# Two chunk slots instead of three, and two projections moved beside the token groups

## The chip, the core and the metric

The kernel runs on one core of a Trainium2 chip. The metric is the device time of one execution in microseconds (us), median of the runs. Five engines work side by side, each through its own instructions in order: TensorE (PE; its weight loads are listed as PEld), VectorE (DVE), ScalarE (ACT), GpSimd (POOL) and SyncE (SP), which here issues nearly all DMAs.

## The reference

One layer of a decoder step for 1024 prompt tokens and 32 sample tokens (T = 1056 columns) of width 1024, in float32:

```python
n1 = rmsnorm(x, norm_mix_g);  z = n1 @ w_in
y_r, shift_new, wkv_new = rwkv7_mix(z[..., :D_SHIFT], ...)
y_p, pool_new = pool_mix(z[..., D_SHIFT:], ...)
h = x + concatenate([y_r, y_p], -1) @ w_out
h = h + peer_ffn(rmsnorm(h, norm_ffn_g), wq, keys, u, v)
gate = sigmoid(rmsnorm(h, norm_ple_g) @ ple_gate_w)
h = h + (p @ ple_w) * gate
y = rmsnorm(h, final_norm_g)
```

`rwkv7_mix` is a recurrence over tokens with an 8-head state. `pool_mix` is a windowed mean with a small projection. `peer_ffn` scores 16384 experts by two sets of 128 keys, takes the top 16 for each of 8 heads, and mixes the rows of `u` and `v`. Besides y the states are returned.

## The kernel before, in words

Matrices are kept transposed: 128 features on the partitions, tokens as columns. A wide float32 product is made of three matmuls in a reduced format: every operand is split into a high part (ScalarE copy) and a low part (raw minus high, on VectorE or GpSimd), and hi x hi, hi x lo and lo x hi are added up (`mm3`, L651).

1. *Projection* (`phase_a`, L195): z for all columns, the factors of the recurrence, which go to DRAM (`fd`), the pooled half `yp_d`, and split copies of `w_out`'s first half and of `wq` to DRAM (`wc_d`).
2. *Chunks* (`bchunk`, L462): the recurrence in 16 chunks of 64 prompt tokens and one sample chunk. A chunk is a generator of 19 steps of small matmuls (64 columns), each followed by a ScalarE, VectorE or GpSimd instruction whose result the next step needs. The state tile S links the chunks. `b_stream` (L915) runs them round robin: at most NSLOT = 3 at a time, each with tiles of its own slot (`wt`, L472, tag with `slot`), a new one not earlier than STAG = 6 rounds after the last. The sample chunk uses slot 1, and chunks of that slot are held back meanwhile (`sample`, L933).
3. *Two more products*. `ple` (L1004): p @ ple_w, 8 blocks of 128 features x 1056 columns in three parts of XW = 352, to `pl_d`, read only near the end of the kernel. `wpool` (L1021): x plus the pooled half's part of w_out, 8 blocks of 3 parts, to `hx_d`, read by each group.
4. *Groups* (`phase_c`, L678): four token groups of 288, 256, 256 and 256 columns (the first has the 32 sample columns and chunks 0 to 3). Per group: load `y_d` (L687) and `hx_d` (L690), 8 blocks of w_out's first half (L699), norm, 16 blocks of wq (L737), keys, scores to DRAM. `wblock` (L637) loads the split weights, three buffers deep.
5. *Top experts* (`top`, `select`, `t_stream`): VectorE searches of the scores of a group, and the build of dense gates for the first 672 columns (L898 to L907: VectorE and GpSimd make one-hot operands, TensorE multiplies them).
6. *Dense experts and the tail*: from about 1410 us on, wide matmuls over all experts (`emm`, L1104), gathers for the other 384 columns beside them, and the last norm.

The order of the work is written by `merge` (L950), which takes the stream that is least far by its length, and a scheduler then places the instructions of that program order by a timeline of its own. Before the change the streams are:

```python
 960 BC = (0, 2, 4, 5, 8, 12, 16)
 976 merge([(16, A), (b_len(*BC[0:2]), b_stream(*BC[0:2]))])
1048 merge([(30, sample(bchunk(-1, ...))), (b_len(*BC[1:3]), b_stream(*BC[1:3]))])
1049 merge([(KB * (1 + T // XW), (x for st in (ple(), wpool()) for x in st)), (b_len(*BC[2:4]), b_stream(*BC[2:4]))])
1124 for step in range(1, NG + 1):   # streams of a step: chunks BC[step+2:step+4], top of group step-2, phase_c(step-1)
```

So step 1 has group 0 beside chunks 5 to 7, step 2 group 1 beside chunks 8 to 11 and the top search of group 0, and so on. PSUM tiles: `PS("b0")` is one ring of four, used by the chunks; `PS("b2")` and `PS("b3")` have two each.

Of the kernel before, what the change touches and what calls it, by code (L numbers as in the profile page):

```python
# [16 lines left out]
ALU = mybir.AluOpType  # L17
# [45 lines left out]
def body(ctx, tc, io):  # L63
# [63 lines left out]
    def PS(tag):  # L127
        return pools[tag].tile([128, 512], F32, name="ps", tag="bc" if tag in ("b0", "b1") else tag)
# [332 lines left out]
    maxn = max(b - a for a, b in GROUPS)  # L461
    def bchunk(c, sp=None):  # L462
        smpl = sp is not None
        slot = 1 if smpl else c % NSLOT
        pst = "b0"
        tt = NSMP if smpl else 64
        ts = slice(NP, T) if smpl else slice(64 * c, 64 * c + 64)
# [2 lines left out]
        msk = mask4 if smpl else mask64  # L470

        def wt(name, n, bufs=1):  # L472
            return pb.tile([128, n], F32, name=name, tag=f"{name}{slot}", bufs=bufs)

        def q4(name, bufs=1):
            return v3(wt(name, 256, bufs), 64)
# [430 lines left out]
            nc.sync.dma_start(g_d[:, :, (col + t1 - GA) // TC].rearrange("g p e t -> p g e t"), st.rearrange("p (g e) t -> p g e t", e=GQ))  # L907

    NG = len(GROUPS)
    NSLOT = 3  # L910
    STAG = 6

    active, nxt, since, held = [], [0], [0], [False]

    def b_stream(ca, cb, ahead=2):  # L915
        while nxt[0] < cb or any(c < cb for c, _ in active):
            c = nxt[0]
            if (c < min(cb + ahead, NCH) and len(active) < NSLOT and (not active or since[0] >= STAG)
                    and not (held[0] and c % NSLOT == 1)):
                active.append((c, bchunk(c)))  # L920
                nxt[0], since[0] = c + 1, 0
            since[0] += 1
            for a in list(active):
                try:
                    next(a[1])
                except StopIteration:
                    active.remove(a)
                yield

    def b_len(ca, cb):  # L930
        return (cb - ca) * 19

    def sample(g):  # L933
        held[0] = True
        yield from g
        held[0] = False

    def t_stream(gi):
        for t0, m in tiles_of(gi):
# [21 lines left out]
    with tc.tile_pool(name="pa1", bufs=1) as pa1:  # L961
# [13 lines left out]
        bzero()  # L975
        merge([(16, A), (b_len(*BC[0:2]), b_stream(*BC[0:2]))])

    with tc.tile_pool(name="smp", bufs=1) as sp_, tc.tile_pool(name="hx", bufs=1) as hx:
        bm = sp_.tile([128, 32], F32, name="bm")
        nc.gpsimd.affine_select(bm, ones[:, 0:32], pattern=[[-NS, 32]], base=0, channel_multiplier=1,  # L980
                                compare_op=ALU.is_ge, fill=0.0)
        nc.gpsimd.affine_select(bm, bm, pattern=[[NS, 32]], base=NS - 1, channel_multiplier=-1,
                                compare_op=ALU.is_ge, fill=0.0)
        bmask = sp_.tile([128, NB], F32, name="bmask")
        TT(bmask, bm[:, 0:NB], bm[:, 16:16 + NB], op=ALU.add)
        cmask = sp_.tile([128, NB, 64], F32, name="cmask")
        nc.gpsimd.memset(cmask, 1.0)
        nc.gpsimd.affine_select(cmask, cmask, pattern=[[-NS, NB], [1, 64]], base=0, channel_multiplier=0,
                                compare_op=ALU.is_ge, fill=0.0)
        nc.gpsimd.affine_select(cmask, cmask, pattern=[[NS, NB], [-1, 64]], base=NS - 1, channel_multiplier=0,  # L990
                                compare_op=ALU.is_ge, fill=0.0)
        ssm = sp_.tile([128, 4, NB, 64], F32, name="ssm")
        nc.sync.dma_start(ssm, io["state_wkv"])
        pT = sp_.tile([128, 2, T], F32, name="pT")
        nc.sync.dma_start(pT, io["p"])

        def split(pool, raw, shape, nm, bufs):
            hi = pool.tile(shape, F32R, name=nm + "hi", bufs=bufs)
            ACT(hi, raw, AF.Copy)
            lo = pool.tile(shape, F32R, name=nm + "lo", bufs=bufs)  # L1000
            TT(lo, raw, hi.bitcast(F32), op=ALU.subtract)
            return hi, lo

        def ple():  # L1004
            phi, plo = split(sp_, pT, [128, 2, T], "p", 1)
            for db in range(KB):
                wp = sp_.tile([128, 2, 128], F32, name="wp", bufs=2)
                nc.sync.dma_start(wp, io["ple_w"][db])
                hi, lo = split(sp_, wp, [128, 2, 128], "w", 2)
                pss = [PS("b3"), PS("b3"), PS("b2")]  # L1010
                for k in range(2):
                    for w, x, first, last in ((hi, phi, k == 0, False), (hi, plo, False, False), (lo, phi, False, k == 1)):
                        for i, ps in enumerate(pss):
                            mm(ps[:, :XW], w[:, k, :], x[:, k, i * XW:(i + 1) * XW], start=first, stop=last)
                for i, ps in enumerate(pss):
                    o = sp_.tile([128, XW], F32, name="pout", bufs=2)
                    ACT(o, ps[:, :XW], AF.Copy)
                    nc.sync.dma_start(pl_d[:, db, i * XW:(i + 1) * XW], o)
                yield

        def wpool():  # L1021
            yhi = hx.tile([128, PB, T], F32R, name="yhi")
            ylo = hx.tile([128, PB, T], F32R, name="ylo")
            for g in range(PB):
                raw = hx.tile([128, T], F32, name="yraw", bufs=1)
                nc.sync.dma_start(raw, yp_d[:, g, :])
                ACT(yhi[:, g, :], raw, AF.Copy)
                TT(ylo[:, g, :], raw, yhi[:, g, :].bitcast(F32), op=ALU.subtract)
            for b in range(KB):
                raw = hx.tile([128, HK, 128], F32, name="wraw", bufs=2)  # L1030
                nc.sync.dma_start(raw, io["w_out"][b, :, HK:, :])
                hi = hx.tile([128, HK, 128], F32R, name="whi", bufs=2)
                ACT(hi, raw, AF.Copy)
                lo = hx.tile([128, HK, 128], F32R, name="wlo", bufs=2)
                TT(lo, raw, hi.bitcast(F32), op=ALU.subtract)
                for i in range(T // XW):
                    cs = slice(i * XW, (i + 1) * XW)
                    x = hx.tile([128, XW], F32, name="x", bufs=3)
                    nc.sync.dma_start(x, io["x"][:, b, cs])
                    ps = PS("b2")  # L1040
                    mm3(ps, [(hi, lo)], (yhi[:, :, cs], ylo[:, :, cs]), XW)
                    TT(x, ps[:, :XW], x, op=ALU.add)
                    nc.sync.dma_start(hx_d[:, b, cs], x)
                    yield

        spf = sp_.tile([128, 28, 64], F32, name="spf")
        nc.gpsimd.memset(spf, 0.0)
        merge([(30, sample(bchunk(-1, ((sp_, ssm), bmask, cmask, spf)))), (b_len(*BC[1:3]), b_stream(*BC[1:3]))])
        merge([(KB * (1 + T // XW), (x for st in (ple(), wpool()) for x in st)), (b_len(*BC[2:4]), b_stream(*BC[2:4]))])


    tk = phases.enter_context(tc.tile_pool(name="tk", bufs=1, reuse_waits="tile"))
    cstack = ExitStack()
    ws = cstack.enter_context(tc.tile_pool(name="ws", bufs=2))
    mv = cstack.enter_context(tc.tile_pool(name="mv", bufs=1))
    work = cstack.enter_context(tc.tile_pool(name="wc", bufs=1))
# [67 lines left out]
    for step in range(1, NG + 1):  # L1124
        streams = []
        if step < NG:
            c_ = BC[step + 2:step + 4]
            streams.append((b_len(*c_), b_stream(*c_)))
        if 0 <= step - 2 < NG:
            streams.append((t_len(step - 2), t_stream(step - 2)))  # L1130
        if 0 <= step - 1 < NG:
            streams.append((CL[step], phase_c(step - 1)))
        if step == NG:
            for _ in streams[0][1]:
                pass
# [4 lines left out]
        merge(streams)  # L1140
# [278 lines left out]
```

## Time and profile before

| what | value |
|---|---|
| median of 3 runs | 3349.01 us (3345.77 to 3352.56) |
| the profiled execution, its own time | 3365.37 us |
| its span | 3363.7 us |
| mean granted TensorE clock | 0.968 |

The span runs from the first to the last instruction of the profiled execution. Its own time is 16.4 us above the median of the runs, so differences are made against the profiled execution and then set on the median. Times in the rows are from the span's start. A matmul's listed duration includes its latency, and matmuls overlap; what one costs in a stream is a stretch divided by its count.

### The profile page before, as it was taken

The numbers are of one execution on the slowest core, as the hardware profiler recorded it, in microseconds if no ns is written. First come the engines' busy times: TensorE is split into PE (matmuls) and PEld (weight loads), VectorE is DVE, ScalarE is ACT, GpSimd is POOL, SyncE is SP. The second block draws the span as 40 slices with busy tenths as digits, with TensorE's granted clock in tenths as the row PEclk, the third lists the DMA queues.
The fourth block names the chain that finished last, engine by engine and source line by source line (L and its number), as shares of the span: only waits on it lengthen the run. The fifth ranks groups of instructions, "written<-read, shape, count | busy, mean of one in ns | idle before, by whom it ended". The sixth has DMA issues, their size and how long they took to land.

```text
span 3363.7 us, 66962 instructions
## 1 busy us (share of the span) xinstructions
PE 3145.6 (94%) x26777; PEld 3006.4 (89%) x26777; DVE 2585.2 (77%) x5124; ACT 1128.8 (34%) x1734; POOL 1736.5 (52%) x1439
## 2 busy tenths in 40 slices
PE   8997799896998988899999999999999999999997
PEld 7886688786787877899999999999999999999997
DVE  6766322229799879899898888888889888888966
ACT  6452322223555555431221222222222222222243
POOL 5433232215446455327666665566566566666634
PEclk9998899997999989999999999999999999999998
DMA  4668544665776796739999999999999999999933
GB/s 160 203 219 195 145 130 127 204 191 149 235 217 201 232 317 204 244 109 371 343 330 332 343 349 328 333 334 339 337 336 349 326 330 342 338 329 337 323 107 127
DMA packets 448856, 879.89 MB, mean 262 GB/s; under 512 B 110240, under 2 KB 233376, under 8 KB 444064
## 3 DMA queue, kind: packets, MB, share of 16 engines
q1 hardware_dynamic: 337952, 472.91, 43.8%
q0 software_dynamic: 110592, 402.70, 32.9%
q8 instruction: 210, 3.44, 0.4%
q14 instruction: 102, 0.84, 0.1%
HBM read 754.89 MB, written 120.60 MB: 260 GB/s over the span
## 4 chain that ended last, share of the span: by engine, by line
PE 54%; DVE 7%; DMA 2%; issue 1%; ACT 0%; POOL 0%; SPq 0%; ACTq 0%; DVEq 0%; POOLq 0%
PE pd L1110 53%; DVE ab L898 1%; DMA row<-u,idx 1%; DVE elo L1088 1%; DVE oh L850 0%; DMA scq<-sc_d 0%; DMA eraw<-wq 0%; DVE OT L1316 0%; DVE ab L899 0%; DVE I L766 0%; DVE s L768 0%; DVE tg L1302 0%; DVE I L770 0%; DMA g_d<-gst 0%; DMA gq<-g_d 0%
## 5 line engine op out<-in xcount | busy, mean ns | idle before, releaser
L1219 POOL DMA_INDIRECT row<-v,idx x384 | 530.6, 1382 | 330.8 <-DVE po L1236 150.9
L1219 POOL DMA_INDIRECT row<-u,idx x384 | 542.5, 1413 | 274.9 <-DVE row L1227 107.4
L1086 ACT ACTIVATE ehi<-eraw 128x1024 fp32r<-128x1024 f32 x278 | 294.5, 1060 | 1095.9 <-PE pd L1110 976.8
L1110 PE MATMUL pd<-XH,elo 128*128 128x336 f32 x2176 | 515.3, 318 | 5.9 <-POOL elo L125 4.7
L1110 PE MATMUL pd<-XL,ehi 128*128 128x336 f32 x2176 | 515.1, 317 | 0.0
L1110 PE MATMUL pd<-XH,ehi 128*128 128x336 f32 x2176 | 512.4, 316 | 0.4 <-ACT ehi L1086 0.4
L1110 PE MATMUL pd<-wh,ehi 128*128 128x336 f32 (+1 forms) x2112 | 504.1, 317 | 6.6 <-DVE tg L1300 6.2
L1110 PE MATMUL pd<-wl,ehi 128*128 128x336 f32 (+1 forms) x2112 | 504.0, 317 | 0.0
L1110 PE MATMUL pd<-wh,elo 128*128 128x336 f32 (+1 forms) x2112 | 503.9, 317 | 0.2 <-DVE elo L1088 0.2
L1236 DVE SCALAR_TENSOR_TENSOR po<-row,act,po 128x1024 f32<-128x1024 f32 x381 | 488.5, 1282 | 6.8
L1227 DVE SCALAR_TENSOR_TENSOR row<-row,xt 128x1024 f32<-128x1024 f32 x384 | 455.7, 1219 | 9.7 <-DMA row<-u,idx 9.5
L1110 PEld LDWEIGHTS pd<-XH,elo 128*128 128x128 f32 x2176 | 373.5, 188 | 7.1 <-POOL elo L125 5.5
L1088 DVE TENSOR_TENSOR elo<-eraw,ehi 128x1024 fp32r<-128x1024 f32 x256 | 318.3, 1243 | 77.2 <-ACT ehi L1086 69.0
L1110 PEld LDWEIGHTS pd<-XH,ehi 128*128 128x128 f32 x2176 | 372.9, 189 | 0.9 <-ACT ehi L1086 0.6
L1110 PEld LDWEIGHTS pd<-XL,ehi 128*128 128x128 f32 x2176 | 371.3, 188 | 0.2
L1110 PEld LDWEIGHTS pd<-wh,ehi 128*128 128x128 f32 x2112 | 362.6, 188 | 7.6 <-issue 7.4
L1110 PEld LDWEIGHTS pd<-wh,elo 128*128 128x128 f32 x2112 | 362.7, 188 | 0.6 <-DVE elo L1088 0.5
L1110 PEld LDWEIGHTS pd<-wl,ehi 128*128 128x128 f32 x2112 | 362.8, 188 | 0.0
L125 POOL TENSOR_TENSOR ab<-ab,e 128x512 f16<-128x512 f16 x110 | 130.1, 1185 | 180.6 <-DVE ab L899 139.0
L657 PE MATMUL ps<-hi,whi 128*128 128x256 f32 (+1 forms) x592 | 185.7, 315 | 29.3 <-DMA whi<-wc_d 15.8
L1179 DVE TENSOR_TENSOR OT<-pd,OT 128x672 f32<-128x672 f32 x120 | 102.9, 857 | 140.7 <-PE pd L1110 139.8
L905 ACT ACTIVATE gst<-ps 128x512 f32<-128x512 f32 x168 | 174.9, 1089 | 85.5 <-PE ps L903 78.4
(428 smaller groups left out, 5526.9 us busy)
## 6 DMA issues: line engine op xcount, KB each, us to landing
eraw<-uT SPq DMA_DIRECT2D x128, 512.0 KB
eraw<-vP SPq DMA_DIRECT2D x128, 512.0 KB
g_d<-gst SPq DMA_DIRECT2D x21, 2048.0 KB
gq<-g_d SPq DMA_DIRECT2D x32, 1344.0 KB
whi<-wc_d SPq DMA_DIRECT2D x148, 256.0 KB
wlo<-wc_d SPq DMA_DIRECT2D x148, 256.0 KB
fdc<-fd SPq DMA_DIRECT2D x16, 896.0 KB
wc_d<-shi SPq DMA_DIRECT2D x40, 256.0 KB
```

The costliest lines, as they stand in the source:

```text
L125: nc.gpsimd.tensor_tensor(out, a, b, op=op)
L657: mm(ps[:, :n], whi[:, kk, :], xhi[:, k, :n], start=k == 0, stop=False)
L898: TT(ab[:, 0:4], iota16[:, None, :, :].to_broadcast([128, 4, EB, 2]), pairs(0, 4), op=ALU.is_equal)
L905: ACT(st[:, :, t2:t2 + 4].rearrange("p e t -> p t e"), v3(ps, 128), AF.Copy, scale=1.0 / GS)
L1086: ACT(hi, raw, AF.Copy)
L1088: sub(lo, raw, hi.bitcast(F32), op=ALU.subtract)
L1110: mm(ps[:, a, :n], w_[:, k, :], x_[:, s:s + n], start=first, stop=last)
L1179: TT(halves(OT[db]), ps[:, :, :NH], halves(OT[db]), op=ALU.add)
L1219: nc.gpsimd.indirect_dma_start(out=r[:m], out_offset=None, in_=io[tab], in_offset=bass.IndirectOffsetOnAxis(ap=idx[:m, hh, k:k + 1], axis=0))
L1227: STT(r[:m], r[:m], 1.0, xt[:m], op0=ALU.mult, op1=ALU.mult, accum_out=pre[:m, k:k + 1])
L1236: STT(po[:m], r[:m], act[:m, k:k + 1], po[:m], op0=ALU.mult, op1=ALU.add)
```

## The change

The slots go from three to two (STAG 6 to 9), and the sample chunk gets tiles of its own, in its own pool. `wpool` takes a list of column ranges, loads and splits its weights in each call with one buffer each, and is called three times: for group 0's columns (256 prompt and 32 sample columns) beside chunk 4, and for prompt columns 256 to 640 and 640 to 1024 in step 1, beside group 0. `ple` takes a column range, splits on GpSimd and is called three times (352 columns each) in step 2, beside group 1. Both use the chunks' PSUM ring. The pools of the groups (`tk`, `ws`, `mv`, `work`) are opened before the pools of the sample chunk and of `wpool`.

```diff
-        slot = 1 if smpl else c % NSLOT
+        slot = "s" if smpl else c % NSLOT
+        own = sp[0][0] if smpl else pb
...
-            return pb.tile([128, n], F32, name=name, tag=f"{name}{slot}", bufs=bufs)
+            return own.tile([128, n], F32, name=name, tag=f"{name}{slot}", bufs=bufs)
...
-    NSLOT = 3
-    STAG = 6
+    NSLOT = 2
+    STAG = 9
...
+    def ple(pl, w0, w1):
+        n = w1 - w0
+        raw = pl.tile([128, 2, n], F32, name="pT")
+        nc.sync.dma_start(raw, io["p"][:, :, w0:w1])
+        x = split(pl, raw, [128, 2, n], "p", 1, PTT)
+        for db in range(KB):
+            wp = pl.tile([128, 2, 128], F32, name="wp", bufs=2)
+            nc.sync.dma_start(wp, io["ple_w"][db])
+            w = split(pl, wp, [128, 2, 128], "w", 2, PTT)
+            ps = PS("b0")
+            for k in range(2):
+                for i, j, first, last in ((0, 0, k == 0, False), (0, 1, False, False), (1, 0, False, k == 1)):
+                    mm(ps[:, :n], w[i][:, k, :], x[j][:, k, :], start=first, stop=last)
+            o = pl.tile([128, n], F32, name="pout", bufs=2)
+            ACT(o, ps[:, :n], AF.Copy)
+            nc.sync.dma_start(pl_d[:, db, w0:w1], o)
+            yield
+
+    def wpool(hx, cols):
...
+        for b in range(KB):
+            raw = hx.tile([128, HK, 128], F32, name="wraw", bufs=1)
+            nc.sync.dma_start(raw, io["w_out"][b, :, HK:, :])
+            w = split(hx, raw, [128, HK, 128], "w", 1)
+            x = hx.tile([128, n], F32, name="x", bufs=2)
+            loads(x, io["x"][:, b, :])
+            ps = PS("b0")
+            mm3(ps, [w], y, n)
+            TT(x, ps[:, :n], x, op=ALU.add)
+            for d, a, b_ in at:
+                nc.sync.dma_start(hx_d[:, b, a:b_], x[:, d:d + b_ - a])
+            yield
+
+    tk = phases.enter_context(tc.tile_pool(name="tk", bufs=1, reuse_waits="tile"))
+    cstack = ExitStack()
+    ws = cstack.enter_context(tc.tile_pool(name="ws", bufs=2))
+    mv = cstack.enter_context(tc.tile_pool(name="mv", bufs=1))
+    work = cstack.enter_context(tc.tile_pool(name="wc", bufs=1))
     with tc.tile_pool(name="smp", bufs=1) as sp_, tc.tile_pool(name="hx", bufs=1) as hx:
...
-        merge([(30, sample(bchunk(-1, ((sp_, ssm), bmask, cmask, spf)))), (b_len(*BC[1:3]), b_stream(*BC[1:3]))])
-        merge([(KB * (1 + T // XW), (x for st in (ple(), wpool()) for x in st)), (b_len(*BC[2:4]), b_stream(*BC[2:4]))])
+        merge([(30, bchunk(-1, ((sp_, ssm), bmask, cmask, spf))), (b_len(*BC[1:3]), b_stream(*BC[1:3]))])
+        merge([(KB, wpool(hx, ((0, GROUPS[0][1] - NSMP), (NP, T)))), (b_len(*BC[2:4]), b_stream(*BC[2:4]))])
...
+        if step == 1:
+            hs = GROUPS[0][1] - NSMP
+            hm = (hs + NP) // 2
+            with tc.tile_pool(name="hx", bufs=1, reuse_waits="tile") as hx:
+                merge(streams + [(2 * KB, (i for c in ((hs, hm), (hm, NP)) for i in wpool(hx, (c,))))])
+        elif step == 2:
+            with tc.tile_pool(name="pl", bufs=1, reuse_waits="tile") as pl:
+                merge(streams + [(3 * KB, (i for w0 in range(0, T, XW) for i in ple(pl, w0, w0 + XW)))])
+        else:
+            merge(streams)
```

## Rows read from the trace of the kernel before

**Rows 1.** The page, span and part 1: busy time, share of the span, instructions

```profile
span 3363.7 us, 66962 instructions
...
PE 3145.6 (94%) x26777; PEld 3006.4 (89%) x26777; DVE 2585.2 (77%) x5124; ACT 1128.8 (34%) x1734; POOL 1736.5 (52%) x1439
```

**Rows 2.** Windows: length, busy us (count) of PE, PEld, DVE, ACT, POOL, clock, DMA

```profile
310.00:372.00 62.00, 48.91 (x780) 42.20 (x778) 26.21 (x34) 18.42 (x39) 21.86 (x22) 0.94 0.68 137
372.00:466.00 94.00, 76.50 (x1444) 70.91 (x1444) 25.69 (x43) 35.16 (x80) 25.61 (x33) 0.89 0.49 141
466.00:567.00 101.00, 101.00 (x1571) 88.85 (x1572) 31.84 (x62) 22.12 (x49) 27.57 (x33) 1.00 0.52 146
567.00:745.00 178.00, 156.52 (x2306) 142.81 (x2301) 41.80 (x154) 49.32 (x114) 39.69 (x52) 0.92 0.67 193
745.00:990.00 245.00, 206.80 (x3004) 180.24 (x3006) 206.31 (x843) 115.72 (x213) 113.40 (x135) 0.92 0.68 196
990.00:1218.00 228.00, 195.44 (x2566) 169.37 (x2562) 205.85 (x759) 119.42 (x195) 113.41 (x123) 0.91 0.78 243
1600.00:1700.00 100.00, 100.00 (x653) 100.00 (x651) 87.51 (x103) 25.77 (x32) 62.61 (x46) 1.00 0.92 337
```

**Rows 3.** TensorE's wide groups in 310 to 372, 372 to 466, 466 to 567 us

```profile
L658 PE MATMUL ps<-xlo,whi 128*128 128x352 f32 x27 | 9.5, 352 | 0.0
L318 PE MATMUL ps<-zr,poolw 128*128 128x352 f32 x18 | 6.9, 496 | 2.4 <-DVE zr L378 2.4
...
L1014 PE MATMUL ps<-phi,whi 128*128 128x352 f32 x48 | 14.8, 364 | 0.0
...
L657 PE MATMUL ps<-yhi,whi 128*128 128x352 f32 x96 | 32.2, 335 | 0.0
```

**Rows 4.** Timeline of the DMA queue: start, length, issue

```profile
521.72 0.90 SPq L635 DMA_DIRECT2D y_d<-yo  x1
...
566.97 0.58 SPq L687 DMA_DIRECT2D y<-y_d  x1
...
739.25 0.53 SPq L635 DMA_DIRECT2D y_d<-yo  x1
...
745.14 0.58 SPq L687 DMA_DIRECT2D y<-y_d  x1
```

**Rows 5.** TensorE's waits (total, times, longest us), 372:466, 567:745, 745:990

```profile
PE ps L486 <- ACT wn L574: 5.6, 2, 3.4
...
PE ps L657 <- DMA whi<-wc_d: 6.8, 2, 6.0
...
PE ps L903 <- DVE ab L899: 9.9, 8, 3.8
PE ps L657 <- ACT hi L683: 4.8, 2, 3.1
PE ps L657 <- DMA whi<-wc_d: 3.5, 3, 1.9
```

**Rows 6.** The DMA queue's own waits, 380 to 575 us

```profile
SPq L1018 <- ACT pout L1017: 40.3, 11, 13.2
```

**Rows 7.** Costs of one: groups of instructions in several stretches, and lines

```profile
L125 POOL TENSOR_TENSOR ltm<-lts,nmt 128x256 f32<-128x256 f32 x23 | 17.0, 748 | 33.8 <-PE ps L486 33.8
...
L125 POOL TENSOR_TENSOR ltm<-lts,nmt 128x256 f32<-128x256 f32 x19 | 16.3, 868 | 23.1 <-PE ps L486 23.1
...
L125 POOL TENSOR_TENSOR slo<-sraw,shi 128x512 fp32r<-128x512 f32 x40 | 66.2, 1656 | 133.7 <-ACT shi L189 120.7 <-PE ps L318 8.3 <-PE ps L232 4.5
...
L1017 ACT ACTIVATE pout<-ps 128x352 f32<-128x352 f32 x24 | 10.2, 457 | 23.2 <-DMA pl_d<-pout 19.0 <-PE ps L1014 4.2
L1033 ACT ACTIVATE whi<-wraw 128x512 fp32r<-128x512 f32 x8 | 5.1, 632 | 12.2 <-PE ps L658 9.7 <-DMA wraw<-w_out 2.5
...
L1039 SPq DMA_DIRECT2D x<-x x24: 327/328/433, 380.7 to 558.6; - x24
L1042 DVE TENSOR_TENSOR x<-ps,x x24: 512/525/525, 476.1 to 564.1; 128x352 f32<-128x352 f32 x24
```

More of the change, by code (lines that the diff above doesn't have):

```diff
@@ L909, in body @@
     NG = len(GROUPS)
-    NSLOT = 3
-    STAG = 6
-    active, nxt, since, held = [], [0], [0], [False]
+    NSLOT = 2
+    STAG = 9
+    active, nxt, since = [], [0], [0]
     def b_stream(ca, cb, ahead=2):
@@ L917, in b_stream @@
             c = nxt[0]
-            if (c < min(cb + ahead, NCH) and len(active) < NSLOT and (not active or since[0] >= STAG)
-                    and not (held[0] and c % NSLOT == 1)):
+            if (c < min(cb + ahead, NCH) and len(active) < NSLOT and (not active or since[0] >= STAG)):
                 active.append((c, bchunk(c)))
@@ L931, in b_len @@
         return (cb - ca) * 19
[L933 to L936, printed above, removed]
     def t_stream(gi):
@@ L976, in body, with split @@
         merge([(16, A), (b_len(*BC[0:2]), b_stream(*BC[0:2]))])
+    def split(pool, raw, shape, nm, bufs, sub=TT):
+        hi = pool.tile(shape, F32R, name=nm + "hi", bufs=bufs)
+        ACT(hi, raw, AF.Copy)
+        lo = pool.tile(shape, F32R, name=nm + "lo", bufs=bufs)
+        sub(lo, raw, hi.bitcast(F32), op=ALU.subtract)
+        return hi, lo
+    def ple(pl, w0, w1):
[15 more added lines that the diff above has]
+            yield
@@ new lines, in wpool, with loads @@
+    def wpool(hx, cols):
+        n = sum(b - a for a, b in cols)
+        at = [(sum(b - a for a, b in cols[:i]), a, b) for i, (a, b) in enumerate(cols)]
+        def loads(o, src):
+            for d, a, b in at:
+                nc.sync.dma_start(o[:, d:d + b - a], src[:, a:b])
+        y = (hx.tile([128, PB, n], F32R, name="yhi"), hx.tile([128, PB, n], F32R, name="ylo"))
+        for g in range(PB):
+            raw = hx.tile([128, n], F32, name="yraw", bufs=1)
+            loads(raw, yp_d[:, g, :])
+            ACT(y[0][:, g, :], raw, AF.Copy)
+            TT(y[1][:, g, :], raw, y[0][:, g, :].bitcast(F32), op=ALU.subtract)
+        for b in range(KB):
[10 more added lines that the diff above has]
+            yield
@@ L993, in body @@
         nc.sync.dma_start(ssm, io["state_wkv"])
[L994 to L1044, printed above, removed]
@@ L1046, in body @@
         spf = sp_.tile([128, 28, 64], F32, name="spf")
         nc.gpsimd.memset(spf, 0.0)
-        merge([(30, sample(bchunk(-1, ((sp_, ssm), bmask, cmask, spf)))), (b_len(*BC[1:3]), b_stream(*BC[1:3]))])
-        merge([(KB * (1 + T // XW), (x for st in (ple(), wpool()) for x in st)), (b_len(*BC[2:4]), b_stream(*BC[2:4]))])
-    tk = phases.enter_context(tc.tile_pool(name="tk", bufs=1, reuse_waits="tile"))
-    cstack = ExitStack()
-    ws = cstack.enter_context(tc.tile_pool(name="ws", bufs=2))
@@ L1055, in body @@
-    mv = cstack.enter_context(tc.tile_pool(name="mv", bufs=1))
-    work = cstack.enter_context(tc.tile_pool(name="wc", bufs=1))
+        merge([(30, bchunk(-1, ((sp_, ssm), bmask, cmask, spf))), (b_len(*BC[1:3]), b_stream(*BC[1:3]))])
+        merge([(KB, wpool(hx, ((0, GROUPS[0][1] - NSMP), (NP, T)))), (b_len(*BC[2:4]), b_stream(*BC[2:4]))])
     gstack = ExitStack()
@@ L1139, in body @@
             streams = [streams[1], (NPRE, upre())]
-        merge(streams)
+        if step == 1:
[8 more added lines that the diff above has]
+            merge(streams)
         if step == NG - 1:
```

## The prediction

> **What bounds the kernel now.** I read the page first: TensorE works 94% of the span [rows 1]. Then the windows by stage. From 1550 us to the end, 1814 us, the kernel is a stream of wide matmuls with TensorE busy all the time (1600 to 1700 us is a sample: 653 matmuls of 336 columns, 100.00 us busy [rows 2]); the change touches nothing there. What it can alter lies between 310 us, where the chunks begin, and the stage of the last group, to 1408 us. There the reader should see two things in [rows 2]: TensorE is never more than about nine tenths busy in a stage except between 466 and 567 us (101.00 of 101.00), and its granted clock is 0.89 to 0.94 where it idles and 1.00 where it doesn't. So the question is not what work is saved (the matmul work stays), but how well TensorE is filled, stage by stage. The waits come third: before group 0 the chunks' small matmuls wait for ScalarE's results; in the stages of groups 0 and 1 the waits are for weights, for ScalarE's splits and for the expert-gate operands on VectorE [rows 5]. The fourth view is the order of issues on the DMA queue [rows 4]: chunk 3's output is stored at 521.72 us, yet group 0 starts to load at 566.97, right after the last addition of the pooled projection at 564.1 [rows 7]; group 1 loads at 745.14, 5.9 us after chunk 7's store at 739.25.
>
> **Terms.** A wide matmul costs 100/653 = 0.153 us at 336 columns [rows 2], 0.456 ns a column; so 0.160 us at 352, 0.131 at 288, 0.175 at 384 (estimates in proportion).
>
> 1. *Out of the stretch 310 to 567.* The ple projection is 8x18 = 144 matmuls (140 of them in the 94 us stage [rows 3]), 23.1 us, and all of it leaves. The pooled projection is 8x3x12 = 288 (three groups of 96 [rows 3]), 46.2 us; 8x12 of 288 columns, 12.6 us, stay and 192 of 384 columns, 33.6 us, leave. TensorE was busy 48.91+76.50+101.00 = 226.4 of 257 us there, 0.88 [rows 2]; 226.4-56.7 = 169.7 are left. With a stagger of nine rounds instead of six and two slots, the next chunks are about half a chunk less far when a stage ends: small matmuls in the stretch are 780-98, 1444-140 and 1571-288-4 (ple's rest), together 3265 [rows 2, 3], for six chunks and the sample chunk, about 480 each; at the 43 ns apiece of the third stage ((101-46.8)/1279, rounded up) a half is 10 us. So 160 us remain. What this takes depends on how dense chunks lie without filler. Bound below: at 0.88 busy 182 us, 75 less. Bound above: the small matmuls after 372 us (1304+1279-240 = 2343) at the rate of 372 to 466, 1304/94 = 13.9 per us, take 168 us: group 0 starts at 540, 27 less. That rate had 23 us of ple matmuls in it; without them 1304/71 = 18.4. Two streams are fewer than three, so I take 16 per us, 146 us, group 0 at 518: **-49**.
>
> 2. *Into the stage of group 0* (178 us): +33.6 us TensorE. Idle there is 21.5 us and the clock 0.92 [rows 2]; the idle sits at weights and at ScalarE's split between the two projections of the group [rows 5], places where an independent matmul can stand in. Bounds: +33.6 (nothing filled) down to 33.6-21.5-4 = +8. I take a little under the middle, **+19**. The slices issue 16 weight loads, 16 of x, 8 of y and 16 stores: 56 at 0.33 us [rows 7] is 19 us of the DMA queue, which lies beside 178 us of other work. ScalarE gets 24 splits at 0.632, VectorE 24 splits and 16 additions at 0.525 to 0.7 (the 352-column addition takes 0.525 [rows 7]): 15 to 28 us on engines at 49.3 and 41.8 of 178, hidden. With one weight buffer a block takes load, split, split and 12 matmuls one after the other, some 0.63+0.7+2.1 us and the load; 16 of these fit into 178 us.
>
> 3. *Into the stage of group 1* (245 us): +23.1 us TensorE, idle 38.2, VectorE at 206.3 [rows 2]. ple uses no VectorE now: its 27 splits go to GpSimd, 24 of 256 elements at 0.75 to 0.87 us and 3 of 704 elements at about 2.3 (1.656 for 512 [rows 7], in proportion), about 27 us on 113.4 of 245: hidden unless GpSimd's part of the expert operands comes late. ScalarE gets 24 outputs at 0.457 [rows 7] and as many smaller splits, under 22 us on 115.7; the queue gets 51 issues, 17 us at 0.33, of 245. Bounds 0 (all in the idle) and +23; taken **+8**, as VectorE and not TensorE is the fuller engine in much of this stage.
>
> 4. *DMA queue.* ple's stores waited at the head of the queue for ScalarE 40.3 us in all [rows 6]. Now behind them stand group 1's weight loads, score loads and chunk loads. The weights are three buffers ahead, which covers most; bounds 0 and +40, taken **+4**.
>
> 5. *Half a chunk repaid* in the last chunk stage, whose TensorE idle is 32.6 us [rows 2]: bounds 0 and +10, taken **+3**. *Pools opened early*: group 0's weights no longer wait for the projection's memory; bounds 0 and -6.0 (the longest wait for weights in group 0's stage [rows 5]), taken **-3**. Fewer slots in the stages of groups 0 to 2 I cost at nothing: a chunk may take twice 61 us in group 1's stage with two slots, and group matmuls cover its waits; without that cover it is rival A.
>
> **Sum:** -49+19+8+4+3-3 = -18. The profiled execution took 3365.4 us, 16.4 above the median of the runs, so 3347 beside it and **3331** on the median.
>
> **Rivals.**
> A, *slower: two chunk chains don't fill TensorE.* Place: 372 us to group 0. It decides if small matmuls run at no more than about 14 per us. For: the 17.5 us idle of 372 to 466 fall into exactly these waits, with three streams and filler present. Against: most of that filler delayed the chains. Term 1 is -27, term 2 +30, term 3 +12, with +4, +3, -3: +19, **3368**.
> B, *VectorE sets the pace from group 1 on.* Then only the shift of group 1's start counts and ple is free: -49+19-3 = -33, **3316**. For: 206 of 245 and of 228 us busy on VectorE [rows 2]. Against: TensorE is at 207 and 195 in the same stages.
> C, *no gain: the idle only moves.* What is freed before group 0 comes back whole behind it (term 2 +33, term 3 +18): about **3349**. For: the trace's idle is made of many waits under 5 us, which any order has.
> D, *GpSimd's new splits hold VectorE up.* A 256-element GpSimd multiply takes 0.748 us before group 0 and 0.868 in group 1's stage, where VectorE is fuller [rows 7]: 16% longer. If they delay VectorE by as long as they run, term 3 is +27 and not +8: +1, **3350**. Against: by the row it is a sixth of 27, 4 us. (The Trainium skill, "SBUF — State Buffer", section "Who interferes with whom", states such a rule: a VectorE instruction with two SBUF inputs and a GpSimd one that reads SBUF shut each other out for the whole instruction. By it the sum would be about 0; the 16% shows much less, so it gets a small chance.)
> E, *the DMA queue is blocked.* ple's stores hold weight loads: term 4 is +40, **3367**. For: 40.3 us of such waits now. Against: the weights' three buffers.
>
> **Numbers.** Chances: forecast 0.36, A 0.18, B 0.20, C 0.10, D 0.06, E 0.10. 0.2% of the time (6.7 us) is about what a measurement of this kernel can tell from no change. Faster: B and nine tenths of the forecast, 0.52; within 0.2%: C, D and the rest of the forecast, 0.20; slower: A and E, 0.28. The forecast's own range is 3316 to 3346. The range for all takes in A and E with 5 us more, and downwards B, with term 1 at -75 and terms 2 and 3 at their lower bounds as its end (-75+8+0+4+3-3 = -63): 3286 to 3373.
>
> **What would show it.** Right: group 0's first load near 518 us and the wait behind the pooled projection gone; group 0's stage about 197 us, at a higher clock and with fewer waits for weights; group 1's stage about 255 us; the wide stream starting some 18 us earlier. Wrong: small matmuls between 372 us and group 0 at 14 per us or fewer with waits for ScalarE longer (A); GpSimd multiplies over 1 us in group 1's stage with VectorE waiting (D); TensorE waits for weight loads above the 6.8 and 3.5 us of now in the stages of groups 0 and 1 [rows 5] with store waits at the head of the queue (E). The whole is wrong if the wide stream starts later than now.

## The result: 3381 us, slower by one per cent

The changed kernel takes 3380.85 us (median of 4 runs, 3375.79 to 3388.40), the kernel before on the same chip 3349.32 (4 runs): a ratio of 1.0097, with a 95% interval from 1.0083 to 1.0112. That is 31.5 us more, and above the range. The two spans differ by 23.0 us only, because the profiled execution of the kernel before took 16.0 us more than this median and that of the changed kernel 7.6 us more; the stages below show where these 23 us are, not all of the 31.5.

The page of the changed kernel, span and busy time, answers to [rows 1]:

```profile
span 3386.7 us, 67243 instructions
...
PE 3151.1 (93%) x26777; PEld 3002.6 (89%) x26777; DVE 2609.0 (77%) x5139; ACT 1147.0 (34%) x1775; POOL 1770.1 (52%) x1466
```

The number of matmuls is the same, 26777. The DMA queue of the changed kernel has the loads of the four groups and the last store of scores (compare [rows 4]):

```profile
480.11 1.21 SPq L688 DMA_DIRECT2D y<-y_d  x1
...
721.55 0.52 SPq L688 DMA_DIRECT2D y<-y_d  x1
...
981.17 0.57 SPq L688 DMA_DIRECT2D y<-y_d  x1
...
1217.43 0.57 SPq L688 DMA_DIRECT2D y<-y_d  x1
...
1430.46 1.22 SPq L748 DMA_DIRECT2D sc_d<-scs  x2
```

The same queue of the kernel before, for the two groups that [rows 4] did not need:

```profile
990.41 0.56 SPq L687 DMA_DIRECT2D y<-y_d  x1
...
1217.89 0.58 SPq L687 DMA_DIRECT2D y<-y_d  x1
...
1407.76 1.22 SPq L747 DMA_DIRECT2D sc_d<-scs  x2
```

Subtract one list from the other. The changed kernel is ahead by 86.9 us at group 0's load, by 23.6 at group 1's, 9.2 at group 2's and 0.5 at group 3's. It is 22.7 us behind at the last scores, and then the wide stream runs as before (1956 us from that store to the end in both). So a large lead is spent stage by stage, and the last stage, in which the diff changes nothing, turns it into a loss.

The windows between these loads (columns as in [rows 2]), changed kernel:

```profile
372.00:480.00 108.00, 85.75 (x2084) 76.92 (x2085) 25.98 (x56) 29.80 (x71) 40.45 (x48) 0.89 0.23 48
480.00:721.60 241.60, 219.15 (x2875) 196.83 (x2873) 76.11 (x211) 70.38 (x156) 47.39 (x59) 0.95 0.74 215
721.60:981.20 259.60, 231.99 (x3216) 201.28 (x3214) 229.83 (x850) 146.33 (x273) 146.09 (x167) 0.96 0.77 229
981.20:1217.40 236.20, 194.06 (x2649) 168.47 (x2645) 188.01 (x793) 103.66 (x185) 103.07 (x121) 0.86 0.67 205
1217.40:1430.50 213.10, 177.67 (x1365) 162.94 (x1365) 177.13 (x614) 102.64 (x140) 108.30 (x89) 0.91 0.72 235
```

The last two stages of the kernel before:

```profile
990.40:1217.90 227.50, 195.03 (x2560) 168.97 (x2554) 205.45 (x758) 119.03 (x195) 113.31 (x123) 0.91 0.78 243
1217.90:1407.80 189.90, 163.02 (x1267) 154.49 (x1267) 159.94 (x654) 93.26 (x131) 97.61 (x89) 0.93 0.76 242
```

Since TensorE is the engine that is nearly always busy, the better question is where it stands (length minus PE busy). Three fixed windows make this comparable between kernels. Kernel before, then changed kernel:

```profile
310.00:570.00 260.00, 229.41 (x3892) 204.94 (x3890) 85.41 (x143) 76.30 (x169) 77.28 (x88) 0.95 0.55 142
570.00:980.00 410.00, 350.81 (x5007) 311.79 (x5003) 238.13 (x964) 156.19 (x313) 145.66 (x181) 0.92 0.67 194
980.00:1500.00 520.00, 460.15 (x4631) 424.33 (x4629) 460.97 (x1903) 256.89 (x388) 230.68 (x244) 0.93 0.69 217
```

```profile
310.00:570.00 260.00, 205.11 (x3849) 182.93 (x3849) 81.80 (x148) 74.07 (x170) 91.77 (x109) 0.89 0.53 130
570.00:980.00 410.00, 374.56 (x5041) 330.44 (x5041) 271.67 (x1004) 186.98 (x361) 164.02 (x192) 0.97 0.77 227
980.00:1500.00 520.00, 440.43 (x4458) 398.74 (x4459) 429.64 (x1738) 230.85 (x360) 221.12 (x227) 0.90 0.64 204
```

TensorE stands 30.6, 59.2 and 59.9 us before, and 54.9, 35.4 and 79.6 us after. Up to 980 us the sums are 89.8 and 90.3: between 570 and 980 us, where the moved projections now run, it stands 24 us less, and before 570 us 24 us more. After 980 us it stands 19.7 us longer.

### The profile page after: what moved, and what is told of

Read it like the earlier page. It is cut to its first block, busy times and chain, and to the rows that moved or that the text cites. A ratio compares the mean times of both kernels' runs of the same rounds, so it can differ in the third digit from the quotient of the medians.

```text
span 3386.7 us, 67243 instructions
## 1 busy us (share of the span) xinstructions
PE 3151.1 (93%) x26777; PEld 3002.6 (89%) x26777; DVE 2609.0 (77%) x5139; ACT 1147.0 (34%) x1775; POOL 1770.1 (52%) x1466
## 4 chain that ended last, share of the span: by engine, by line
PE 66%; DVE 15%; DMA 7%; issue 2%; POOL 2%; ACT 1%; SPq 1%; ACTq 0%; DVEq 0%; POOLq 0%
PE pd L1104 53%; PE ps L487 5%; DVE ab L899 2%; PE ps L658 2%; PE ps L660 2%; PE ps L659 2%; DMA sraw<-wq 2%; DVE ab L900 1%; DMA whi<-wc_d 1%; DVE oh L851 1%; PE ps L904 1%; DMA wlo<-wc_d 1%; DMA scq<-sc_d 1%; DMA yraw<-yp_d 1%; DVE h L715 1%
## 5 line engine op out<-in xcount | busy, mean ns | idle before, releaser
L1082 DVE TENSOR_TENSOR elo<-eraw,ehi 128x1024 fp32r<-128x1024 f32 x256 | 317.4, 1240 | 75.7 <-ACT ehi L1080 70.0
L658 PE MATMUL ps<-hi,whi 128*128 128x256 f32 (+1 forms) x592 | 185.3, 314 | 35.9 <-DMA whi<-wc_d 20.1
```

Of the source, the lines that this page charges most:

```text
L658: mm(ps[:, :n], whi[:, kk, :], xhi[:, k, :n], start=k == 0, stop=False)
L1082: sub(lo, raw, hi.bitcast(F32), op=ALU.subtract)
```

## The experiments

In the table "standing" is TensorE's length minus busy time in the three windows above, from each kernel's profile, and the last column is its ratio to the kernel before measured beside it, with the 95% interval. 0.001 is 3.3 us. A row's standing is that of one execution, whose own time lies 16 us above the kernel's median for the kernel before, 10 us for e1, 8 us for the changed kernel and within 7 us for the others.

| run | kernel | 310:570 | 570:980 | 980:1500 | ratio |
|---|---|---|---|---|---|
| | before | 30.6 | 59.2 | 59.9 | 1 |
| | changed | 54.9 | 35.4 | 79.6 | 1.0097 [1.0083, 1.0112] |
| e1 | slots alone | 41.7 | 53.0 | 80.3 | 1.0096 [1.0079, 1.0113] |
| e2 | slots, pooled slices | 50.6 | 48.2 | 64.2 | 1.0068 [1.0051, 1.0085] |
| e3 | slots, ple slices | 41.6 | 45.0 | 68.1 | 1.0027 [1.0011, 1.0042] |
| e4 | changed, pools late | 44.7 | 40.3 | 75.8 | 1.0063 [1.0047, 1.0080] |
| e5 | changed, search last | 59.4 | 34.6 | 78.9 | 1.0089 [1.0072, 1.0106] |
| e6 | e1, search last | 34.5 | 54.3 | 80.8 | 1.0078 [1.0061, 1.0094] |
| e7 | before, search last | 33.3 | 52.8 | 74.1 | 1.0075 [1.0058, 1.0092] |
| e8 | e3, search last | 39.3 | 47.9 | 71.4 | 1.0074 [1.0057, 1.0091] |
| e9 | changed, search as before | 57.3 | 35.6 | 64.3 | 1.0060 [1.0047, 1.0074] |
| e10 | e3, search as before | 37.7 | 46.7 | 55.4 | 1.0013 [1.0002, 1.0024] |
| e11 | slots, starts 6 apart | 27.4 | 47.9 | 74.9 | 1.0034 [1.0024, 1.0044] |
| e12 | changed, group 3 first | 56.1 | 33.0 | 80.2 | 1.0124 [1.0109, 1.0140] |
| e13 | changed, starts 6 apart | 48.3 | 47.7 | 82.3 | 1.0119 [1.0102, 1.0135] |
| e14 | e3, starts 6 apart | 37.3 | 44.7 | 79.4 | 1.0059 [1.0045, 1.0073] |
| e15 | e14, group 3 first | 36.3 | 40.9 | 81.4 | 1.0080 [1.0066, 1.0094] |
| e16 | e4, search as before | 45.0 | 33.4 | 61.8 | 1.0014 [1.0005, 1.0023] |
| e17 | e11, search as before | 28.7 | 47.0 | 57.4 | 0.9974 [0.9963, 0.9986] |
| e18 | changed, starts 8 apart | 50.6 | 40.1 | 83.1 | 1.0124 [1.0108, 1.0139] |

**Which part costs: e1 to e4.** e1 is the kernel before with the first hunks of the diff (two slots, starts nine steps apart, the sample chunk's own tiles). e2 adds the pooled projection's three slices to it, e3 ple's; e4 is the changed kernel with the groups' pools opened where they were.

```diff
# e1
-    NSLOT = 3
-    STAG = 6
+    NSLOT = 2
+    STAG = 9
# e4
-    tk = phases.enter_context(tc.tile_pool(name="tk", ...))   # ahead of the sample chunk
...
+    tk = phases.enter_context(tc.tile_pool(name="tk", ...))   # ahead of gstack, as before
```

> The kernel before with two chunk slots, STAG 9 and own tiles for the sample chunk, both projections where they were. Theory S (two chains leave TensorE idle before group 0): most of the change's +32 us is here, +20 to +35 us. Theory P (ple beside group 1 delays VectorE's top search, and the delay comes out in group 3's stage) and theory W (slices of the pooled projection beside group 0 cost what they free): -5 to +10 us, as the two projections fill the gaps between the chunks.

> As e1, and the pooled projection in three slices, two of them beside group 0 (ple where it was before). Theory W: +20 us or more over e1. Theory S: within 8 us of e1. Theory P: within 8 us of e1.

> As e1, and ple in three slices beside group 1 (the pooled projection whole, where it was before). Theory P: +20 us or more over e1, with VectorE waiting for scores between 1100 and 1230 us. Theory S and W: within 8 us of e1.

> The changed kernel with the groups' pools opened after the sample chunk's, as before; all else of the change in. If the early pools cost nothing: +32 us, like the changed kernel. If their place in memory makes the wait (group 0's tiles no longer where the sample's were): +10 us or less.

The slots alone cost as much as the whole change (1.0096 against 1.0097), as S said; P and W expected a moved projection to cost time, and it gives some back (the letters P and W stand for other theories further down). Either projection moved alone gives back 9 us (e2, at the edge of noise) or 23 us (e3), both together 11 us with the pools late (e4) and nothing with the pools early. So opening the pools early, costed at a gain of 3 us, loses 11: the standing ahead of 570 us goes from 44.7 to 54.9 (e4's +21 us on the kernel before lies between its two branches). What e2 and e3 gain cannot be put down to the projections alone. The traces show that the scheduler also put the last part of VectorE's search for group 2 elsewhere: behind the 115th one-hot set in e1 and the 114th in e4 and the changed kernel, but behind the 130th in e2 and the 132nd in e3, and 16.1 and 12.2 us of the standing that goes are after 980 us. What this place does is tested below. The last two stages of e1 show that the loss of its profile lies wholly behind group 3's load, and not before group 0, where S had it:

```profile
985.60:1215.80 230.20, 191.47 (x2666) 167.83 (x2665) 188.57 (x771) 105.42 (x187) 101.30 (x122) 0.88 0.70 210
1215.80:1436.80 221.00, 181.99 (x1363) 167.51 (x1364) 179.31 (x636) 100.74 (x139) 106.16 (x89) 0.89 0.70 229
```

It reaches that load 2.1 us ahead of the kernel before and then takes 221.0 us, not 189.9. Three slots with either projection moved were not tried.

**Theory V, the order on VectorE: e5 to e8.** VectorE takes its instructions in order, and the scheduler writes that order anew for each kernel. Group 2's search is four quads (a quad is one load of scores with four searches in it); 168 one-hot sets (L898 and L899, each for the gates of four columns) stand in the same queue, 136 of them for groups 0 and 1. The kernel before has the quads behind the 104th, 104th, 112th and 136th set, the changed kernel behind the 99th, 104th, 107th and 114th. VectorE's waits between 990 and 1240 us, changed kernel and then the kernel before:

```profile
DVE V L766 <- DMA scq<-sc_d: 25.5, 3, 22.0
DVE S L612 <- PE ps L487: 6.9, 1, 6.9
```

```profile
DVE ab L898 <- PE ps L903: 23.8, 10, 13.7
DVE S L611 <- PE ps L486: 3.8, 1, 3.8
DVE V L765 <- DMA scq<-sc_d: 3.6, 1, 3.6
```

And the place in the changed kernel's timeline of VectorE:

```profile
1129.39 0.41 DVE L901 TENSOR_TENSOR ab<-ab,e 128x512 f16<-128x512 f16 x1
1151.79 0.87 DVE L766 MAX8 V<-scq 128x8 f32<-128x128 f32 x4 [21.98 <-DMA scq<-sc_d]
```

It stands 22 us at a search whose scores have not come, with one-hot sets queued behind. V says that this is the loss. The first test puts all four quads, and what follows from them, behind the 136th set, in four kernels:

```diff
-                TT(ab[:, 4:6], ab[:, 2:4], pairs(2, 2), op=ALU.mult)
+                lastab[0] = TT(ab[:, 4:6], ab[:, 2:4], pairs(2, 2), op=ALU.mult).ins
...
+            with tc.issue_after(lastab[0]):
                 for _ in streams[0][1]:
                     pass
```

> The changed kernel, with VectorE's search of group 2 queued behind the last one-hot set of group 1. Theory V (the loss is VectorE standing in its own order for group 2's scores, 25.5 us between 990 and 1240 us, with group 1's one-hots behind it): the wait goes below 8 us and the kernel is 15 to 25 us faster than the changed one, +8 to +17 us on the kernel before. Theory S (two chunk chains leave TensorE idle): no change, +32 us, within 7 us.

> As e1 (two slots alone), with the same order on VectorE. Theory V: +10 to +20 us on the kernel before, from +32. Theory S: +32 us, within 7.

> The kernel before (three slots), with the same order on VectorE. There that wait is 3.6 us. Theory V: within 8 us of the kernel before. If a later search of group 2 by itself costs more than the wait: +10 us or more.

> As e3 (two slots, ple beside group 1, pooled projection whole), with the same order on VectorE. Theory V: the 21.1 us wait goes and 15 to 20 us come off e3's +9: -5 to -12 us on the kernel before, faster than both. Theory S: +9 us as e3.

The wait for scores is gone (0.2 us in e5), but the numbers of V failed. Those of S come out in e5 and e6 (by the ratios +30 and +26 us on the kernel before), not in e8. The kernel before loses 25 us, e8 loses 16 against e3, and all four come out between 1.0074 and 1.0089, whatever their slots and projections. So the order matters by itself, and the last place is about as bad as the early one: the last gates are then stored at 1410.6 us in e5, not 1382.0.

**The search where the kernel before has it: e9 to e11.**

```diff
+    QP = (104, 104, 112, 136)
...
+                abl.append(TT(ab[:, 4:6], ...).ins)   # each one-hot set in turn
...
+            with (tc.issue_after(abl[QP[i // 4] - 1]) if qn[0] == 2 else ExitStack()):   # group 2 alone
                 nc.vector.max(v8[:, 0:8], s_)
...
# e11: this alone, on e1
-    STAG = 9
+    STAG = 6
```

> The changed kernel with group 2's four search quads held on VectorE behind the 104th, 104th, 112th and 136th one-hot set, where the kernel before has them (the changed kernel has them behind the 99th, 104th, 107th and 114th). Theory V (VectorE, which takes its instructions in order, stands at a search whose scores have not come, 25.5 us between 990 and 1240 us, while one-hot sets lie ready behind it): the wait for scores falls below 8 us, fewer than 42 sets are left when group 3's load is issued, and the time falls by 12 to 26 us to 3355 to 3369 us. Rival T (with two slots the last chunks run alone, so VectorE has nothing else to do between 1100 and 1200 us, whatever its order): the wait turns into one for the last chunk's state on TensorE, VectorE stays below 62 of 100 us there, and the time stays within 6 us of 3381 us.

> Two slots and the ple projection beside group 1's chunks, pooled projection in its old place, with the same four positions of group 2's search as the kernel before. Theory V: the 20 us of waits for scores go, and the time is 3335 to 3348 us, at or below the kernel before (3349 us; 3361 us without the positions). Rival T: within 6 us of 3361 us, VectorE below 68 of 100 us between 1100 and 1200 us.

> Two slots and the sample chunk's own tiles alone, with the chunk starts 6 steps apart as in the kernel before, not 9. Its build has group 2's search behind the 98th, 107th, 107th and 114th set, much as with 9 (97, 107, 108, 115). Theory V: the time stays within 8 us of 3386 us. Rival T, or the stagger of 9 itself as the cost: 15 us or more come back, 3371 us or less.

The traces have the quads at these places or a few sets behind (the third behind the 113th in e9, the second and third behind the 107th and 113th in e10). By the ratios e9 comes out 12 us below the changed kernel and e10 5 us below e3, which is not clear of noise (the intervals overlap): V's direction, short of its numbers, and in e9 more than T allowed. But V's reason falls with it: VectorE still waits 15.9 us for scores in e9, twice what V allowed. What shrank is seen on TensorE. Its waits for one-hot operands between 980 and 1500 us, changed kernel and then e9 (whose L908, L904 and L905 are L904, L900 and L901 of the changed kernel):

```profile
PE ps L904 <- DVE ab L900: 23.4, 24, 3.1
PE ps L904 <- DVE ab L901: 10.8, 11, 2.1
PE ps L658 <- DMA whi<-wc_d: 10.6, 4, 5.4
```

```profile
PE ps L908 <- DVE ab L904: 10.6, 11, 2.5
...
PE ps L908 <- DVE ab L905: 8.2, 6, 2.1
```

34.2 us become 18.8. As the waits for GpSimd's part of these operands and for ScalarE's copies of the gates grow, all waits before one-hot matmuls fall from 45.4 to 35.9 us, and those before the group's matmuls from 23.0 to 13.7 us; all standing after 980 us falls by 15.3. e11, where the search stays early, shows that the stagger of nine is itself a good part of the slots' cost, as its second branch said: 21 us of e1's 32 come back, and 14.3 of the 24.8 us by which the standing falls lie ahead of 570 us.

**Two more guesses, both wrong: e12 to e15.** Theory P: the adds of h that group 3 needs are queued behind one-hot sets, so its head is late. Rival Q: starts nine steps apart are the cost everywhere.

```diff
# e12, e15
+            for _ in range(KB + 1):
+                next(streams[1][1])        # group 3's first steps
             for _ in streams[0][1]:        # group 2's search, selection, one-hot sets
                 pass
# e13, e14, e15
-    STAG = 9
+    STAG = 6
```

> The changed kernel with the first nine steps of group 3 (its output projection, down to the store of hT_d) written ahead of group 2's search and one-hot sets; its build then has the eight adds of h behind the 130th to 136th set, not the 130th to 141st. Theory P (in every run so far the span ends 1956 us after the last store of group 3's scores, or 1973 us after the last gate store, whichever is later; and after group 3's load VectorE's queue has one-hot sets ahead of the adds that group 3 needs): load to hT_d falls from 69 us to 60 or less, the last score store comes 8 to 16 us earlier than 1430 us, and the time is 3364 to 3373 us. Rival Q (the chunk starts 9 steps apart alone make the last chunk late): within 5 us of 3381 us.

> The changed kernel with chunk starts 6 steps apart, nothing else. Rival Q, and P as far as group 3's load comes earlier: what 6 steps gave the slots alone (24 us of 3386) comes back here too: 3354 to 3366 us, with group 3's load near 1190 us instead of 1217. Against both: with the slices beside them the chunks cannot use the closer starts, and the time stays above 3374 us. Under P the end of the span is again the last score store plus 1956 us, or the last gate store plus 1973 us.

> Two slots, chunk starts 6 steps apart, only the ple projection moved. Theory P and rival Q: the two gains add (25 us of ple's move, 24 us of 6 steps), less what the adds of h lose behind the 135th to 142nd set: 3337 to 3350 us, at or below the kernel before. If the gains do not add: 3356 us or more.

> The same with the first nine steps of group 3 ahead of group 2's search; the adds of h then stand behind the 135th to 139th set. Theory P: 5 to 12 us below that run, 3328 to 3343 us, with load to hT_d at 62 us or less. Rival Q: within 4 us of it.

P and Q both missed. In e12 the time from group 3's load to the store of hT_d, the end of its output projection, falls to 60.9 us and the last scores come at 1412.7, about as P said, yet the time rises by 9 us. Only 264 of the experts' wide matmuls now run ahead of that store, where the changed kernel has 409; the other 145, at the 0.153 us of the prediction, are 22 of the 24 us by which the stretch behind the store grew (1980 against 1956). A landmark moved is no time gained as long as TensorE stands as long (80.2 against 79.6 us). e13 takes the branch against both: the starts that gave e1 21 us back give the changed kernel nothing (7 us more, at the edge of the two intervals). In e14 the gains do not add either: the same starts cost e3 11 us. There the search shows why: the scheduler has its last quad behind the 114th set, where e3 has it behind the 132nd, and the standing falls by 4.6 us up to 980 us and rises by 11.3 behind. So the best stagger depends on what lies beside the chunks and on the order that is written behind them. e15 against e14 repeats e12 (264 matmuls against 409).

**Theory W, TensorE's standing time is the account: e16 to e18.** The edits are those of e4 and e9 together, of e11 and e9 together, and STAG = 8 in the changed kernel.

> The changed kernel with the groups' pools opened after the sample chunk (alone: 3372.6 us) and with group 2's search at the kernel before's places (alone: 3371.3 us, from 3380.9 us). Theory W (TensorE's standing time before the wide stream is what the time adds up, and these two edits take it out of different stages): both gains come together, 3358 to 3367 us; standing between 310 and 570 us near 45, after 980 us near 64 (as 44.7 and 64.3 in the two alone). Rival X (what one gives, the other would have given): 3369 us or more.

> Two slots with chunk starts 6 steps apart, nothing moved, with group 2's search at the kernel before's places. Theory W: standing between 310 and 980 us stays near 75 us (the kernel before: 89.8), after 980 us it falls from 75 us to 55 to 66 us, and the time is 3342 to 3354 us (3361.9 us without the places). Rival X (here the sets wait 14.8 us for ScalarE's gates, and a search held back leaves VectorE nothing to do meanwhile): 3360 us or more.

> The changed kernel with chunk starts 8 steps apart instead of 9; the same instructions. Theory W: no direction is foretold, but the change of the time against 3380.9 us is that of TensorE's standing time before 1500 us and of what its clock loses, within 8 us. If the time stays within 3 us, one step of the stagger does not matter; if it moves by 8 us or more, the stagger's size is one of the things that a change of slots has to be tuned with.

e16 and e17 went as W said (e16 one microsecond below its range): the two edits of e16 add up, out of different windows. e17, nothing moved, two slots, starts six apart, and four search quads put in place, is the only kernel faster than the kernel before (0.9974). Its search stands where the kernel before has it, so it is the fair comparison of two slots with three. Its three windows:

```profile
310.00:570.00 260.00, 231.28 (x3670) 205.73 (x3672) 81.11 (x143) 75.38 (x169) 76.68 (x94) 0.94 0.58 153
570.00:980.00 410.00, 363.03 (x5334) 320.21 (x5330) 280.26 (x1124) 174.72 (x332) 162.84 (x198) 0.93 0.71 202
980.00:1500.00 520.00, 462.61 (x4643) 428.73 (x4642) 444.46 (x1757) 245.78 (x373) 221.67 (x231) 0.92 0.67 213
```

28.7, 47.0 and 57.4 us of standing are 1.9, 12.2 and 2.5 us below the kernel before, whose row is of an execution 16 us above its median, so only the second is clear. X falls by 17 us. Here VectorE waits longer for scores than in e11 (17.8 against 9.6 us) and the kernel is 20 us faster, so the length of that wait does not decide. In e18 TensorE stands 3.9 us longer up to 1500 us and the time is 12 us higher (9 by the ratios): 8.3 us apart (5 by the ratios), at the edge of what W allowed. The two profiled executions are within 0.5 us of each other, so the traces do not show those 9 to 12 us. One step of the stagger seems to move this kernel by 0.3%, though the two intervals just touch, and there is no theory of the direction.

## Why the prediction was wrong

**Terms 1 and 2, right together, wrong apart.** Group 0's load came at 480 us, not 518, and its stage took 241.6 us, not 197; together the lead at group 1's load was 23.6 us where the terms gave 30. The border shifted because TensorE work that term 1 left ahead of group 0's load ran behind it. Term 1 kept the first pooled slice (96 matmuls of 288 columns) ahead of the load; 84 of them ran behind it, as the changed kernel's matmuls between 480 and 567 us show:

```profile
L658 PE MATMUL ps<-yhi,whi 128*128 128x288 f32 x28 | 9.4, 335 | 2.2 <-ACT whi L975 2.2
L660 PE MATMUL ps<-yhi,wlo 128*128 128x288 f32 x28 | 9.0, 322 | 0.0
L659 PE MATMUL ps<-ylo,whi 128*128 128x288 f32 x28 | 8.9, 319 | 0.0
```

The three groups overlap, so their times do not add up: without these 84, TensorE would be busy 13.5 us less in the stage. And the chunks were further behind than the half chunk, about 240 small matmuls, of term 1: between 310 us and the load 2732 of them ran (L487), 531 fewer than before (3263, L486), and in group 0's stage 2010, 289 more (1721 before). By the traces TensorE's busy time in the stage grew by 62.6 us (156.5 to 219.2): 51.4 of it are the pooled matmuls, the 192 of 384 columns included, and 11.2 the rest, which the 289 small matmuls account for (12.4 us at the prediction's 43 ns). Term 2 let 14.6 of the slices' 33.6 us vanish into idle time, but the stage stands 22.5 us as it stood 21.5 before; all of it was paid.

**Term 3** gave 8 us, measured 14.3 (259.6 against 245.3), within its bounds. **Term 4** was small as forecast: TensorE's waits for high weights in group 0's stage are 2.7 us, where they were 6.8, and 6.8 us in group 1's, where they were 3.5 [rows 5]; ple's stores hold up the queue for ScalarE 8.0 us in all, not 40.3 [rows 6]. **Pools early**, taken at -3, had the wrong sign: they cost 11 us (e4), and with the pools late group 1's load comes at 703.2 us, 41.9 us ahead. So the nearness of 23.6 to the 30 of terms 1 and 2 was in part luck. At group 2's load 9.2 us of lead are left, where the sum had 18 by then with its queue term.

**The step that failed** is term 5, in two of its parts. One is the sign of the early pools. The larger one is "Fewer slots in the stages of groups 0 to 2 I cost at nothing", with 3 us for the half chunk repaid and no term at all for group 3. Groups 2 and 3 cost 8.7 and 23.2 us, 31.9 together where the sum had 3; that is 29 of the 41 us between the forecast of 18 us less and the span of 23 us more. e1 has the same standing after 980 us with neither projection moved (80.3 against 79.6), so the projections are not needed for it; nor do the slots bring it by themselves, as e2 and e3, with the same slots and stagger, stand 64.2 and 68.1 us. What goes with it is the place of group 2's search (below). Of the 19.7 us more of standing there, TensorE's waits by consumer show 12.7 in front of group matmuls (the largest rise by 5 to 6 us each: high weights, 5.6 to 10.6, and the adds of h at L701, from none to 5.6), 5.6 in front of chunk matmuls, 4.7 in front of one-hot matmuls and 3.5 less before the rest. I had looked for a cover of the chunks' waits in the stage where the slots act, and not asked how the scheduler would write the stages behind it.

**The rivals.** A's time (3368) was nearest, but not its condition: the small matmuls from 372 to 480 us run at (2084-12)/108 = 19.2 per us, not 14. C, "the idle only moves", is right to half a microsecond up to 980 us (89.8 and 90.3), in part by luck, as with the pools late the sum is 85.0 (e4); it has nothing for the loss behind. B fails: group 1's stage, which it left as long as it was, grew, with TensorE busy 232.0 and VectorE 229.8 of 259.6 us. D fails by its own sign: GpSimd's 256-element multiply takes 870 ns there, as before [rows 7], and the new splits of 256 elements 805 ns; so the lock rule of the Trainium skill ("SBUF — State Buffer", "Who interferes with whom") again shows little of its full size. E fails by term 4: the waits for weights grew by 3.3 us in group 1's stage, not by 40.

**What is shown and what stays open.** Shown, in four pairs of kernels whose sources differ in nothing but the place of group 2's search (e9, e10, e16, e17 against the changed kernel, e3, e4, e11): standing after 980 us falls by 15.3, 12.7, 14.0 and 17.5 us, and the time by 12, 5, 16 and 20 us, clear of noise in all but the second. With the pools opened late besides, e16 is at 1.0014: the early pools and the place of the search account for 28 of the change's 32 us, and without them the two slots and the moved projections together still gain nothing (5 us more). The 20 traces agree. Where the first three quads stand behind the 97th to 113th set and the last behind the 130th or later (the kernel before, e2, e3, e9, e10, e16, e17), standing after 980 us is 55.4 to 68.1 us. Where the last stands behind the 114th or 115th, it is 74.9 to 83.1 us, and with all four behind the 136th (e5 to e8) 71.4 to 80.8 us. The windows of the changed kernel and then of e9 suggest why:

```profile
1200.00:1250.00 50.00, 29.22 (x202) 23.28 (x201) 49.52 (x203) 24.04 (x32) 28.62 (x27) 0.62 0.85 290
1350.00:1400.00 50.00, 37.03 (x294) 34.04 (x293) 25.32 (x67) 20.14 (x25) 15.89 (x14) 0.90 0.86 274
```

```profile
1200.00:1250.00 50.00, 37.66 (x266) 32.97 (x263) 33.64 (x58) 25.61 (x31) 28.54 (x22) 0.65 0.95 320
1350.00:1400.00 50.00, 42.99 (x358) 40.58 (x357) 47.98 (x172) 26.16 (x33) 30.96 (x22) 0.86 0.72 223
```

With the search early, VectorE (the third busy time) is full when TensorE needs one-hot sets and half idle later. This is a reading, not a test: the scheduler also writes other orders anew behind the moved search, of ScalarE, GpSimd and the DMA queue, and no run holds those still. Shown as well is that nine steps of stagger cost the two slots 21 us when nothing is moved. Not settled is why starts nearer together do not help the changed kernel (e13, e18, where the last quad stays behind the 114th or 115th set), and which instruction of the scheduler's order makes the waits for weights longer. e1 with the search of the kernel before was not run.

## What to carry to other kernels

Where one engine is nearly always busy, add up its standing time stage by stage for before and after: over these 20 kernels the sum of the three windows goes with the ratio at a correlation of 0.93, while the start of a single group says little (from -0.5 for group 0's load to 0.4 for group 3's). Moving filler from one stage to another gains only if the stage that gives it up has other work to show; here one lost 24 us and the other gained 24, 10 of the loss by the early pools. And whatever changes a stage changes the order that a scheduler writes for the stages behind it, so compare the places of the late consumers (here four search quads among 168 sets) before believing that a part of a change costs or gains anything.

## What the hardware did that I had not expected

A stretch of waits is paid twice on TensorE, in the waits and in slower matmuls. Right after 1200 us, when it waits for one-hot operands, its windows in the kernel before and then in the changed kernel are:

```profile
1200.00:1225.00 25.00, 16.33 (x109) 14.44 (x109) 13.33 (x23) 12.00 (x14) 12.30 (x9) 0.64 1.03 356
1225.00:1250.00 25.00, 25.00 (x204) 24.54 (x203) 17.92 (x70) 13.77 (x20) 14.35 (x17) 1.00 0.86 266
```

```profile
1200.00:1225.00 25.00, 12.04 (x88) 8.50 (x87) 25.00 (x118) 11.55 (x14) 12.78 (x15) 0.50 1.03 365
1225.00:1250.00 25.00, 17.18 (x115) 14.79 (x115) 24.52 (x86) 12.49 (x19) 15.84 (x12) 0.73 0.67 215
```

With 12 of 25 us busy the granted clock is 0.50, the lower of its two levels (1.2 GHz), for the whole window; in the ten us before, TensorE was busy 6.8 us. In these 50 us 203 matmuls are done where the kernel before did 313, but they are not of the same kinds, and the larger part of the loss is waits. The clock's part is seen on the one-hot matmuls, in the kernel before from 1225 to 1250 us, at 1.00, and in the changed kernel from 1200 to 1225 us, at 0.50:

```profile
L903 PE MATMUL ps<-ab 128*128 128x128 f16 x48 | 3.4, 219 | 0.0
```

```profile
L904 PE MATMUL ps<-ab 128*128 128x128 f16 x88 | 12.4, 304 | 13.2 <-DVE ab L900 6.6 <-POOL ab L125 5.4 <-DVE ab L901 0.7
```

One is listed with 219 ns at the higher clock and 304 ns at the lower, and 13.2 us of the 25 are waits.
